# Gates of a token mixer in pairs by seven block products, branch by branch

## The chip, the cores and the metric

The kernel runs on one core of a Trainium2 chip. The core has a matrix engine (TensorE, PE), a vector engine (VectorE, DVE), a scalar engine (ScalarE, ACT), GpSimd (POOL) and a queue engine (SyncE, SP) that here issues DMAs. The metric is device time in microseconds (us). The kernel before takes 2490.34 us, the median of three runs (2489.82 to 2491.25).

## The reference

Two layers over 512 tokens of width 1024, all in 32-bit floats. Each layer is a gated feed-forward block, a token mixer, and a second feed-forward block, each followed by a layer norm. The mixer has three attention branches (a: sparse attention with compressed, selected and windowed keys; b: a sliding window with sinks; c: attention with forget gates), each 512 wide, whose outputs are projected, gated and summed:

```python
q_a, kv_a, g_a, q_b, k_b, v_b, q_c, k_c, v_c, f_c = _split_cols(h @ w_in)
o_a, o_b, o_c = _nsa(...), _swa_sink(...), _fox(...)
g = jax.nn.sigmoid(h @ w_gate + b_gate).reshape(B, S, N_BRANCH, D)
merged = g[:, :, 0] * (o_a @ w_br_a) + g[:, :, 1] * (o_b @ w_br_b) + g[:, :, 2] * (o_c @ w_br_c)
return merged @ w_out
```

`h` is 512 x 1024, `w_gate` 1024 x 3072, each `w_br` 512 x 1024, `w_out` 1024 x 1024. The feed-forward block is `(silu(x @ w1[:, :F]) * (x @ w1[:, F:])) @ w2` with F = 2816.

## The kernel before

**Products of three parts.** A 32-bit operand is held as two parts, `hi` (ACT copies the raw tile to a rounded format) and `lo` (DVE subtracts `hi` from the raw tile). A product of two such operands is three matmuls: hi by hi, hi by the other's lo, lo by hi (`mm3`, L169 to L171). Weights come by DMA on SP into a raw tile 128 x 1024 (`wraw`, three buffers) and are split by `wsplit` (L148 on ACT, L149 on DVE) into a pair of tiles `hi`, `lo` (`unit`: three pairs in the pool `wt`, two more in `wx` where that is open, two more in the feed-forward stage). Activations lie transposed, `xh` and `xl`: 8 planes of 128 features by 512 tokens. A chunk, 128 output columns over all 512 tokens, is 8 planes x 3 = 24 matmuls of 512 columns (`proj`).

**Feed-forward by seven products.** Most column blocks f of the feed-forward stage take their two chunks (gate and up) together. Tokens are cut in two halves and features in two halves; the two chunks are the rows of a 2 x 2 block product, computed with seven block products in place of eight (`seven` and `strassen`). `seven` (L284) loads both chunks' raw tiles `rg` and `ru`, forms sums of halves in two tiles `ws` on DVE (L298 to L301), and splits `rg` (`ug`), the two sums (`u1`, `u2`) and one half of `ru` (`dh`, `dl`). `token_sums` forms the four sums of token halves once per stage and splits them into `th`, `tl`. `strassen` runs the seven products, each 4 planes x 3 matmuls of 256 columns (L361), in three PSUM banks; between them ACT copies a bank to `sn` (L368), and DVE makes the sums `v`, the second chunk `u` and the last addition into the bank (L372 to L380).

**The tail of the mixer.** While the attention runs, gate chunks fill PE between its parts (`chunk`, `pump`): five of each layer's 24, the first block of all three branches (their Tanh goes to `gates0`) and the second block of branches a and b, whose banks are `held`. After the attention comes the tail (L1173 to L1224). The outputs of the three branches are split into `oh`, `ol` (L1208, L1209; 12 tiles each). Then, for each of the 8 blocks d of 128 columns, the three gates (24 matmuls and a Tanh each, L1090; sigmoid is written as a Tanh), and for the branches b, c, a in turn the branch product (`brp`, 4 planes x 3 = 12 matmuls of 512 columns), the gating `(t + 1) * p` on DVE (L1220) and the addition to the block's sum (L1222). The sum is split at once into plane d of `mh` and `ml`, which the product with `w_out` reads (`rows_ln`, L182 to L184): first with planes 0 to 3 over all tokens, then with the other four.

**What sets the order.** PE's and POOL's instructions stand in the order in which the program writes them. Those of DVE, ACT and SP are put in order by a scheduler that sees the whole program; each engine then works strictly through its own list. Buffers are handed on by semaphores: a tile may be written when its slot's last reader is done. SP issues the DMAs of its list one after the other, each when its target is free. [...]

Of the kernel before, what the change touches and what calls it, by code (L numbers as in the profile page):

```python
# [64 lines left out]
def body(tc, a, out, depth=DEPTH):  # L65
# [49 lines left out]
    def wraw(shape=None):  # L115
        return wt.tile(list(shape or [P, KD, P]), F32, name="raw", tag="raw", bufs=3)
# [164 lines left out]
    def ffn_first(w1):  # L281
        return [wcols(w1, c) for c in (0, F, P, F + P)]

    def seven(w1, f):  # L284

        v = w1.rearrange("(k p) f -> p k f", p=P)
        rg = wraw()
        ru = nx.w1.tile([P, KD, P], F32, name="raw", tag="raw") if f % 2 else wraw()  # L290
        nc.sync.dma_start(rg, v[:, :, f * P:(f + 1) * P])
        nc.sync.dma_start(ru, v[:, :, F + f * P:F + (f + 1) * P])
        ug, u1, u2 = wsplit(rg), unit(), unit()
        ud = [nx.w1.tile([P, 4, P], F32R, name=n, tag=n) for n in ("dh", "dl")]
        h1, h2 = slice(0, 4), slice(4, 8)
        x1, x2 = [nx.w1.tile([P, KD, P], F32, name="ws", tag="ws", bufs=2) for _ in range(2)]
        tt = nc.vector.tensor_tensor
        tt(x1[:, h1], ru[:, h1], ru[:, h2], op=OP.add)  # L298
        tt(x1[:, h2], x1[:, h1], rg[:, h1], op=OP.subtract)  # L299
        tt(x2[:, h1], rg[:, h1], ru[:, h1], op=OP.subtract)  # L300
        tt(x2[:, h2], rg[:, h2], x1[:, h2], op=OP.subtract)  # L301
        for (hi, lo), x in ((u1, x1), (u2, x2)):
            nc.scalar.activation(hi, x, AF.Copy)  # L303
            tt(lo, x, hi.bitcast(F32), op=OP.subtract)  # L304
        nc.scalar.activation(ud[0], ru[:, h2], AF.Copy)
        tt(ud[1], ru[:, h2], ud[0].bitcast(F32), op=OP.subtract)
        return ug, u1, u2, ud

    def token_sums(st):

# [17 lines left out]
    def ffn(l, w1, w2, which, xap, xa, wts, pend, done_prev, last, nxt):  # L328
# [20 lines left out]
        H1, H2 = slice(0, 256), slice(256, 512)  # L349

        def strassen(f, ws):
            (ug, u1, u2, ud), (t1, t2, t3, t4) = ws, st.t
            ga, pa, pb = ps(name="pg"), ps(name="pu"), ps(name="pv")
            p_, r_, s_ = [(xh[:, k:k + 4, c], xl[:, k:k + 4, c]) for k, c in ((0, H1), (4, H1), (4, H2))]

            def prod(o, w, k0, x, first=True):
                for k in range(4):
                    hi, lo = w[0][:, k0 + k], w[1][:, k0 + k]
                    vh, vl = x[0][:, k], x[1][:, k]
                    for i, (wx, vx) in enumerate(((hi, vh), (hi, vl), (lo, vh))):  # L360
                        nc.tensor.matmul(o, wx, vx, start=first and k == 0 and i == 0, stop=k == 3 and i == 2,  # L361
                                         skip_group_check=True)

            tt = nc.vector.tensor_tensor
            prod(ga[:, H1], ug, 0, p_)
            prod(ga[:, H2], u1, 0, t1, False)
            sn = st.w1p.tile([P, S], F32, name="sn", tag="sn", bufs=2)
            nc.scalar.activation(sn, ga, AF.Copy)  # L368
            prod(pa[:, H1], u1, 4, t2)
            prod(pa[:, H2], u2, 0, t3, False)  # L370
            v = st.w1p.tile([P, S], F32, name="v", tag="v", bufs=2)
            tt(v[:, H1], pa[:, H1], sn[:, H1], op=OP.add)  # L372
            tt(v[:, H2], pa[:, H2], v[:, H1], op=OP.add)
            prod(pb[:, H1], ud, 0, t4)
            u = hpart(f)
            tt(u[:, H1], pb[:, H1], v[:, H2], op=OP.add)
            tt(u[:, H2], sn[:, H2], v[:, H2], op=OP.add)
            prod(ga[:, H1], ug, 4, r_, False)
            prod(ga[:, H2], u2, 4, s_, False)
            tt(ga[:, H2], ga[:, H2], v[:, H1], op=OP.add)  # L380
            evac(f, ga, u)
# [15 lines left out]
        for f in range(2, KF):  # L397
            if f == KF - 1:
                for k, n in enumerate(("hi", "lo")):
                    h_parts(k, wt.tile([P, KD, P], F32R, name=n, tag=n, bufs=3)  # L400
                            .rearrange("p (a b) c -> p a (b c)", a=2))
            if f not in PLAIN:
                strassen(f, seven(w1, f))
# [70 lines left out]
    def mix(l, wts, pend, done_ffn, xap, xa, nxt):  # L474
# [499 lines left out]
        def chunk(c0, then, w=w_in, load=wcols, bank="mm"):  # L974
            st = K()

            def part(i):
                def go():
                    if i == 0:
                        st.w = load(w, c0)  # L980
                        st.p = ps(bank, "pj")
                    proj(st.p, st.w, ks=range(i, i + 1))
                    if i == 7:
                        then(st.p)
                return go

            fill.extend(part(i) for i in range(8))
# [101 lines left out]
        def gate_ev(t, p, br, d):  # L1089
            nc.scalar.activation(t, p, AF.Tanh, scale=0.5, bias=bg[:, br, d:d + 1])  # L1090

        def gate_chunk(br):
            chunk(br * D, lambda p: gate_ev(gates0[br], p, br, 0), a["w_gate"][l])
# [85 lines left out]
        oh = [[None] * 4 for _ in range(3)]  # L1179
        ol = [[None] * 4 for _ in range(3)]  # L1180
        for br in (1, 2, 0):
            for i in range(4):
                oh[br][i] = ohp.tile([P, S], F32R, name=f"oh{br}{i}")
                ol[br][i] = ohp.tile([P, S], F32R, name=f"ol{br}{i}")
        def wbr(d, brs):
            r = wraw()
            for j, br in enumerate(brs):
                nc.sync.dma_start(r[:, 4 * j:4 * j + 4],
                                  wb[br].rearrange("(k p) f -> p k f", p=P)[:, :, d * P:(d + 1) * P])
            return wsplit(r[:, 0:4 * len(brs)], 4 * len(brs))  # L1190

        def gates(d):
            g_t = []
            for br in range(3):
                if d == 1 and br < 2:
                    p = held[br]
                else:
                    p = ps("sc" if d == 1 else None, "gate")
                    proj(p, wcols(a["w_gate"][l], br * D + d * P))
                t = tp_.tile([P, S], F32, name="t", tag="t", bufs=4)  # L1200
                gate_ev(t, p, br, d)
                g_t.append(t)
            return g_t

        g_1 = gates(1)
        for br in (1, 2, 0):
            for i in range(4):
                nc.scalar.activation(oh[br][i], o_t[br][i], AF.Copy)  # L1208
                nc.vector.tensor_tensor(ol[br][i], o_t[br][i], oh[br][i].bitcast(F32), op=OP.subtract)  # L1209
        for d in range(KD):  # L1210
            g_t = gates0 if d == 0 else g_1 if d == 1 else gates(d)
            for br in (1, 2, 0):
                if br != 2:
                    w = wbr(d, (1, 2) if br else (0,))
                k0 = 4 if br == 2 else 0
                p = ps(name="brp")
                for k in range(4):
                    mm3(p, w, k0 + k, oh[br][k], ol[br][k], k == 0, k == 3)
                t = g_t[br]
                nc.vector.scalar_tensor_tensor(t, t, 1.0, p, op0=OP.add, op1=OP.mult)  # L1220
                if br != 1:
                    nc.vector.tensor_tensor(g_t[1], g_t[1], t, op=OP.add)  # L1222
            nc.scalar.activation(mh[:, d], g_t[1], AF.Copy)
            nc.vector.tensor_tensor(ml[:, d], g_t[1], mh[:, d].bitcast(F32), op=OP.subtract)  # L1224
        ohp.release()
        op.release()
        xap2, xa2 = alloc_xa()
# [146 lines left out]
```

## Time and profile before

| what | value |
|---|---|
| median of 3 runs | 2490.34 us |
| the profiled execution | 2489.96 us, of which the span from first to last instruction is 2488.3 us |
| PE busy | 2470.7 us, 15691 matmuls |
| DVE busy | 1639.8 us |
| ACT busy | 1121.1 us |
| granted TensorE clock | 0.999 |
| tail of the first layer | 683.13 to 851.94 us of the span, 168.81 us |
| feed-forward stage by seven products, first of four | 61.31 to 242.73 us, 181.42 us |

A row of the groups view has the line, engine, operation, output and inputs, shape and count, then busy time in us and the mean of one in ns, then the engine's idle time just before it and what ended it. A row of the waits view has the engine and line that waited, what it waited for, us in total, times, and the longest. A row of the stage table has the stretch in us from the span's start, its length, then each engine's busy time with its instructions, the granted clock, the DMA share and GB/s. A timeline row has the start, the length and the instruction. Matmuls are pipelined and overlap in the record, so it is the distance between starts that counts.

### The profile page before, as it was taken

The page shows a single profiled execution, that of the slowest core. Times are in us where ns is not written, and L with a number is a line of the kernel's source. Part 1 is how long each engine was busy: PE and PEld are TensorE (multiplying, and loading weights), DVE is VectorE, ACT ScalarE, POOL GpSimd, SP SyncE. Part 2 cuts the span into 40 slices and gives each one's busy share as a digit, 9 for nine tenths or more (in the row PEclk, how much of TensorE's full clock was granted, in tenths as well). Part 3 has the DMA queues.
Part 4 walks back from the last instruction along what each step waited for, and adds up shares of the span by engine and source line. Part 5 has one row for each costly group of instructions (what it writes and reads, how often), then busy time and mean ns, then how long its engine had stood idle before and what let it go on. Part 6 is the DMA issues. An engine that isn't in the chain of part 4 may idle for free.

```text
span 2488.3 us, 40610 instructions
## 1 busy us (share of the span) xinstructions
PE 2470.7 (99%) x15691; PEld 2185.0 (88%) x15691; DVE 1639.8 (66%) x3353; ACT 1121.1 (45%) x2148; POOL 228.5 (9%) x454
## 2 busy tenths in 40 slices
PE   9999999999999999999999999999999999999998
PEld 8999887788888889998899998878888888899986
DVE  7897355587654388984579963566776434889734
ACT  4444234577642344443334442345666323444421
POOL 2000110133300000000000000002332000000000
PEclk9999999999999999999999999999999999999999
DMA  6334443633143333334333343445321534333431
GB/s 207 102 102 140 155 128 116 174 86 90 42 141 102 122 122 94 109 111 144 110 102 111 102 160 94 134 120 148 98 77 36 158 95 143 103 102 103 136 119 60
DMA packets 378098, 286.19 MB, mean 115 GB/s; under 512 B 17464, under 2 KB 349384, under 8 KB 377904
## 3 DMA queue, kind: packets, MB, share of 16 engines
q1 hardware_dynamic: 370496, 258.68, 35.6%
q0 software_dynamic: 7408, 24.90, 2.6%
q8 instruction: 124, 2.03, 0.3%
q14 instruction: 70, 0.57, 0.1%
HBM read 256.22 MB, written 17.88 MB: 110 GB/s over the span
## 4 chain that ended last, share of the span: by engine, by line
PE 97%; DVE 2%; DMA 1%; issue 0%; ACT 0%; SPq 0%; DVEq 0%; POOLq 0%; POOL 0%; ACTq 0%
PE pg L361 17%; PE pu L361 8%; PE acc L183 8%; PE acc L184 8%; PE acc L182 8%; PE pj L169 5%; PE pj L170 5%; PE pj L171 5%; PE pv L361 4%; PE gate L169 3%; PE gate L170 3%; PE gate L171 3%; PE brp L169 2%; PE brp L170 2%; PE brp L171 2%; PE sN L888 2%
## 5 line engine op out<-in xcount | busy, mean ns | idle before, releaser
L149 DVE TENSOR_TENSOR lo<-raw,hi 128x1024 fp32r<-128x1024 f32 (+2 forms) x342 | 401.5, 1180 | 478.7 <-ACT hi L148 464.2
L148 ACT ACTIVATE hi<-raw 128x1024 fp32r<-128x1024 f32 (+2 forms) x342 | 347.4, 1023 | 602.1 <-PE acc L183 233.2
L169 PE MATMUL pj<-xh,hi 128*128 128x512 f32 (+1 forms) x720 | 266.9, 371 | 0.4 <-ACT hi L148 0.4
L171 PE MATMUL pj<-xh,lo 128*128 128x512 f32 (+1 forms) x720 | 254.5, 354 | 0.0
L170 PE MATMUL pj<-xl,hi 128*128 128x512 f32 (+1 forms) x720 | 254.4, 353 | 0.1
L182 PE MATMUL acc<-hi,hs 128*128 128x512 f32 x640 | 249.5, 390 | 0.0
L184 PE MATMUL acc<-lo,hs 128*128 128x512 f32 x640 | 249.0, 389 | 0.0
L183 PE MATMUL acc<-hi,hs 128*128 128x512 f32 x640 | 249.0, 389 | 0.0
L361 PE MATMUL pg<-xh,lo 128*128 128x256 f32 x864 | 244.5, 283 | 0.0
L361 PE MATMUL pg<-xl,hi 128*128 128x256 f32 x864 | 244.5, 283 | 0.0
L361 PE MATMUL pg<-xh,hi 128*128 128x256 f32 x864 | 244.5, 283 | 0.0
L303 ACT ACTIVATE hi<-ws 128x1024 fp32r<-128x1024 f32 x144 | 151.9, 1058 | 138.2 <-DVE ws L299 41.5
L304 DVE TENSOR_TENSOR lo<-ws,hi 128x1024 fp32r<-128x1024 f32 x144 | 175.6, 1221 | 29.5 <-ACT hi L303 29.0
L361 PEld LDWEIGHTS pg<-xl,hi 128*128 128x128 f32 x864 | 165.9, 192 | 0.2
L361 PEld LDWEIGHTS pg<-xh,hi 128*128 128x128 f32 x864 | 165.9, 192 | 0.2
L361 PEld LDWEIGHTS pg<-xh,lo 128*128 128x128 f32 x864 | 165.9, 192 | 0.0
L361 PE MATMUL pu<-th,hi 128*128 128x256 f32 x576 | 163.0, 283 | 0.0
L361 PE MATMUL pu<-tl,hi 128*128 128x256 f32 x576 | 163.0, 283 | 0.0
L361 PE MATMUL pu<-th,lo 128*128 128x256 f32 x576 | 163.0, 283 | 0.0
L171 PEld LDWEIGHTS pj<-xh,lo 128*128 128x128 f32 x720 | 136.1, 189 | 19.7
L169 PEld LDWEIGHTS pj<-xh,hi 128*128 128x128 f32 x720 | 136.4, 189 | 16.2 <-issue 3.7
L170 PEld LDWEIGHTS pj<-xl,hi 128*128 128x128 f32 x720 | 136.8, 190 | 11.7 <-DVE xl L1319 0.3
(324 smaller groups left out, 5873.3 us busy)
## 6 DMA issues: line engine op xcount, KB each, us to landing
raw<-in_ffn_w_dram SPq DMA_DIRECT2D x264, 512.0 KB, 3.8
raw<-in_w_in_dram SPq DMA_DIRECT2D x56, 512.0 KB, 3.9
raw<-in_w_gate_dram SPq DMA_DIRECT2D x48, 512.0 KB, 4.0
x_sp<-xa POOLq DMA_DIRECT2D x24, 512.0 KB, 5.8
ks<-hl SPq DMA_DIRECT2D x96, 128.0 KB, 2.4
xa<-x_sp POOLq DMA_DIRECT2D x16, 512.0 KB, 6.3
raw<-in_w_out_dram SPq DMA_DIRECT2D x16, 512.0 KB, 3.6
tab<-bvec SPq DMA_DIRECT2D x16, 256.0 KB, 3.9
```

The source lines that it names most:

```text
L148: nc.scalar.activation(hi[:, c], raw[:, c], AF.Copy)
L149: nc.vector.tensor_tensor(lo[:, c], raw[:, c], hi[:, c].bitcast(F32), op=OP.subtract)
L169: nc.tensor.matmul(o, hi[:, k], vh, start=first, stop=False)
L170: nc.tensor.matmul(o, hi[:, k], vl, start=False, stop=False)
L171: nc.tensor.matmul(o, lo[:, k], vh, start=False, stop=last)
L182: nc.tensor.matmul(o, sh(k)[:, t], hi[:, c], start=k == 0, stop=False)
L183: nc.tensor.matmul(o, sl(k)[:, t], hi[:, c], start=False, stop=False)
L184: nc.tensor.matmul(o, sh(k)[:, t], lo[:, c], start=False, stop=k == nk - 1)
L303: nc.scalar.activation(hi, x, AF.Copy)
L304: tt(lo, x, hi.bitcast(F32), op=OP.subtract)
L361: nc.tensor.matmul(o, wx, vx, start=first and k == 0 and i == 0, stop=k == 3 and i == 2, skip_group_check=True)
L888: nc.tensor.matmul(o[:, 0:nb].rearrange("p k b j -> p (k b j)"), q, kx[:, 2 * b0:2 * (b0 + nb)].rearrange("p a b -> p (a b)"), start=i == ...
```

## The change

The order of the tail becomes branch by branch: all eight blocks of branch b, then of c, then of a. A sum `mf` (8 planes) collects the gated products; `oh` and `ol` hold one branch at a time (`o_split`). Branch b's eight gates stay whole chunks: the first five are the attention's fillers now (three with their Tanh in `gates0`, two `held`), three stand in the tail. Branches c and a, 16 chunks of each layer's 24, go in pairs of neighbouring blocks through the seven products that the feed-forward stage uses; `strassen` is made general for it (`seven_products`, with the pool and the number of buffers of `sn` and `v` as arguments; two in the feed-forward stage as before, one in the tail). The token sums of `xh`, `xl` are formed in four parts (`token_sums_k`) between branch b's products, and their parts `th`, `tl` lie in the tiles `mh`, `ml`, which take the split merged sum only at the end (`merged`). One raw tile now carries two blocks of one branch's weights (`wbr`), where it carried one block of two branches.

```diff
-    def seven(w1, f):
-        v = w1.rearrange("(k p) f -> p k f", p=P)
+    def seven(w, ca, cb, pl, ru):
+        v = w.rearrange("(k p) f -> p k f", p=P)
         rg = wraw()
-        ru = nx.w1.tile([P, KD, P], F32, name="raw", tag="raw") if f % 2 else wraw()
-        nc.sync.dma_start(rg, v[:, :, f * P:(f + 1) * P])
-        nc.sync.dma_start(ru, v[:, :, F + f * P:F + (f + 1) * P])
+        nc.sync.dma_start(rg, v[:, :, ca:ca + P])
+        ru = ru or wraw()
+        nc.sync.dma_start(ru, v[:, :, cb:cb + P])
         ug, u1, u2 = wsplit(rg), unit(), unit()
...
+    def seven_products(ws, t, pl, u, nb):
+        (ug, u1, u2, ud), (t1, t2, t3, t4) = ws, t
+        ga, pa, pb = ps(name="pg"), ps(name="pu"), ps(name="pv")
...
+        prod(ga[:, H1], ug, 0, p_)
+        prod(ga[:, H2], u1, 0, t1, False)
+        sn = pl.tile([P, S], F32, name="sn", tag="sn", bufs=nb)
+        nc.scalar.activation(sn, ga, AF.Copy)
+        prod(pa[:, H1], u1, 4, t2)
+        prod(pa[:, H2], u2, 0, t3, False)
+        v = pl.tile([P, S], F32, name="v", tag="v", bufs=nb)
+        tt(v[:, H1], pa[:, H1], sn[:, H1], op=OP.add)
+        tt(v[:, H2], pa[:, H2], v[:, H1], op=OP.add)
+        prod(pb[:, H1], ud, 0, t4)
+        tt(u[:, H1], pb[:, H1], v[:, H2], op=OP.add)
+        tt(u[:, H2], sn[:, H2], v[:, H2], op=OP.add)
+        prod(ga[:, H1], ug, 4, r_, False)
+        prod(ga[:, H2], u2, 4, s_, False)
+        tt(ga[:, H2], ga[:, H2], v[:, H1], op=OP.add)
+        return ga
...
-        for br in range(3):
-            gate_chunk(br)
-        for br in range(2):
-            chunk(br * D + P, held.append, a["w_gate"][l])
+        for d in range(3):
+            gate_chunk(d)
+        for d in (3, 4):
+            chunk(D + d * P, held.append, a["w_gate"][l])
...
+        oh = [ohp.tile([P, S], F32R, name=f"oh{i}") for i in range(4)]
+        ol = [ohp.tile([P, S], F32R, name=f"ol{i}") for i in range(4)]
+        mf = ohp.tile([P, KD, S], F32, name="mf")
+        th, tl = (x.rearrange("p (i a) (b s) -> p i (a b) s", a=2, b=2) for x in (mh, ml))
+        tsum = [(th[:, i], tl[:, i]) for i in range(4)]
+        def token_sums_k(k):
...
+            tt(x, xk[0], xk[1], op=OP.add)
+            p_, q, r_, s_ = x[:, 0, H1], x[:, 0, H2], x[:, 1, H1], x[:, 1, H2]
+            for i, u, v in ((0, q, p_), (1, s_, t[:, 0]), (2, s_, q), (3, r_, t[:, 1])):
+                tt(t[:, i], u, v, op=OP.subtract)
+            nc.scalar.activation(th[:, :, k], t, AF.Copy)
+            tt(tl[:, :, k], t, th[:, :, k].bitcast(F32), op=OP.subtract)
...
+        def gate_pair(br, d):
+            ws = seven(a["w_gate"][l], br * D + d * P, br * D + (d + 1) * P, ohp, None)
+            u = g_t[br, d + 1] = gtile()
+            p = seven_products(ws, tsum, ohp, u, 1)
+            gate_ev(u, u, br, d + 1)
+            gate(br, d, p)
+        def branch(br, d, w):
+            p = bank("brp")
+            for k in range(4):
+                mm3(p, w, 4 * (d % 2) + k, oh[k], ol[k], k == 0, k == 3)
+            t = g_t.pop((br, d))
+            o = mf[:, d] if br == 1 else t
+            nc.vector.scalar_tensor_tensor(o, t, 1.0, p, op0=OP.add, op1=OP.mult)
+            if br != 1:
+                nc.vector.tensor_tensor(mf[:, d], mf[:, d], t, op=OP.add)
...
+        gate(1, 5)
+        o_split(1)
+        for d in (3, 4):
+            gate(1, d, held[d - 3])
+        branches(1, 0)
+        token_sums_k(0)
+        gate(1, 6)
+        token_sums_k(1)
+        branches(1, 2)
+        gate(1, 7)
+        token_sums_k(2)
+        branches(1, 4)
+        token_sums_k(3)
+        branches(1, 6)
+        for br in (2, 0):
+            for d in range(0, KD, 2):
+                gate_pair(br, d)
+                if d == 0:
+                    o_split(br)
+                if (br, d) == (0, KD - 2):
+                    merged(range(KD - 2))
+                branches(br, d)
+        merged((KD - 2, KD - 1))
```

More of the change, by code (lines that the diff above doesn't have):

```diff
@@ L307, in seven, with prod @@
         return ug, u1, u2, ud
+    def seven_products(ws, t, pl, u, nb):
+        (ug, u1, u2, ud), (t1, t2, t3, t4) = ws, t
+        ga, pa, pb = ps(name="pg"), ps(name="pu"), ps(name="pv")
+        p_, r_, s_ = [(xh[:, k:k + 4, c], xl[:, k:k + 4, c]) for k, c in ((0, H1), (4, H1), (4, H2))]
+        def prod(o, w, k0, x, first=True):
+            for k in range(4):
+                hi, lo = w[0][:, k0 + k], w[1][:, k0 + k]
+                vh, vl = x[0][:, k], x[1][:, k]
+                for i, (wx, vx) in enumerate(((hi, vh), (hi, vl), (lo, vh))):
+                    nc.tensor.matmul(o, wx, vx, start=first and k == 0 and i == 0, stop=k == 3 and i == 2,
+                                     skip_group_check=True)
+        tt = nc.vector.tensor_tensor
+        prod(ga[:, H1], ug, 0, p_)
[14 more added lines that the diff above has]
+        return ga
     def token_sums(st):
@@ L347, in h_parts @@
             hs[k] = t
[L349 to L381, printed above, removed]
         pts = staged(wts, pend)
@@ L402, in ffn @@
             if f not in PLAIN:
-                strassen(f, seven(w1, f))
+                ru = nx.w1.tile([P, KD, P], F32, name="raw", tag="raw") if f % 2 else None
+                ws = seven(w1, f * P, F + f * P, nx.w1, ru)
+                evac(f, seven_products(ws, st.t, nx.w1, hpart(f), 2), hpart(f))
                 continue
@@ L1178, in mix @@
         ohp = pool("ohp", reuse_waits="tile")
-        oh = [[None] * 4 for _ in range(3)]
-        ol = [[None] * 4 for _ in range(3)]
-        for br in (1, 2, 0):
+        oh = [ohp.tile([P, S], F32R, name=f"oh{i}") for i in range(4)]
[3 more added lines that the diff above has]
+        tsum = [(th[:, i], tl[:, i]) for i in range(4)]
@@ new lines, in token_sums_k @@
+        def token_sums_k(k):
+            tt = nc.vector.tensor_tensor
+            x, t = (ohp.tile([P, KD, P], F32, name="ws", tag="ws", bufs=2) for _ in range(2))
+            x = x.rearrange("p (b k) s -> p b (k s)", b=2)
+            t = t.rearrange("p (i k) s -> p i (k s)", i=4)
+            xk = [y.rearrange("p (b k) s -> p k b s", b=2)[:, k].bitcast(F32) for y in (xh, xl)]
+            tt(x, xk[0], xk[1], op=OP.add)
[4 more added lines that the diff above has]
+            tt(tl[:, :, k], t, th[:, :, k].bitcast(F32), op=OP.subtract)
@@ L1182, in mix, with o_split, wbr @@
+        def o_split(br):
             for i in range(4):
-                oh[br][i] = ohp.tile([P, S], F32R, name=f"oh{br}{i}")
-                ol[br][i] = ohp.tile([P, S], F32R, name=f"ol{br}{i}")
-        def wbr(d, brs):
+                nc.scalar.activation(oh[i], o_t[br][i], AF.Copy)
+                nc.vector.tensor_tensor(ol[i], o_t[br][i], oh[i].bitcast(F32), op=OP.subtract)
+        def wbr(br, d):
             r = wraw()
[L1187 to L1224, printed above, removed]
+            v = wb[br].rearrange("(k p) f -> p k f", p=P)
@@ new lines, in wbr, with bank, gtile, gate @@
+            for j in range(2):
+                nc.sync.dma_start(r[:, 4 * j:4 * j + 4], v[:, :, (d + j) * P:(d + j + 1) * P])
+            return wsplit(r)
+        g_t = {(1, d): gates0[d] for d in range(3)}
+        early = deque(["sc", "tp", "sc", "tp", "sc"])
+        def bank(name):
+            return ps(early.popleft() if early else None, name)
+        def gtile():
+            return tp_.tile([P, S], F32, name="t", tag="t", bufs=4)
+        def gate(br, d, p=None):
+            if p is None:
+                p = bank("gate")
+                proj(p, wcols(a["w_gate"][l], br * D + d * P))
+            t = g_t[br, d] = gtile()
+            gate_ev(t, p, br, d)
@@ new lines, in gate_pair @@
+        def gate_pair(br, d):
[6 more added lines that the diff above has]
+            p = bank("brp")
+            for k in range(4):
+                mm3(p, w, 4 * (d % 2) + k, oh[k], ol[k], k == 0, k == 3)
[4 more added lines that the diff above has]
+                nc.vector.tensor_tensor(mf[:, d], mf[:, d], t, op=OP.add)
@@ new lines, in branches, with merged @@
+        def branches(br, d):
+            w = wbr(br, d)
+            branch(br, d, w)
+            branch(br, d + 1, w)
+        def merged(ds):
+            for d in ds:
+                nc.scalar.activation(mh[:, d], mf[:, d], AF.Copy)
+                nc.vector.tensor_tensor(ml[:, d], mf[:, d], mh[:, d].bitcast(F32), op=OP.subtract)
+        gate(1, 5)
[5 more added lines that the diff above has]
+        gate(1, 6)
```

9 lines of the change are left out of this document (5 added, 4 removed).

## The prediction

> **What bounds the kernel now.** I read the page's busy shares first, then the list of what TensorE (PE) waited for over the whole run.
>
> ```profile
> PE 2470.7 (99%) x15691; PEld 2185.0 (88%) x15691; DVE 1639.8 (66%) x3353; ACT 1121.1 (45%) x2148; POOL 228.5 (9%) x454
> ...
> PE xT L1316 <- DMA xa<-in_x_dram: 4.7, 1, 4.7
> PE ptS L778 <- ACT p L519: 0.9, 2, 0.5
> PE cum L607 <- DVE p L517: 0.7, 2, 0.3
> PE pj L169 <- ACT hi L148: 0.4, 1, 0.4
> PE pt L226 <- issue: 0.3, 1, 0.3
> ```
>
> PE waits 7.0 us in 2488.3, and 4.7 of that is the input at the start. So time is set by how many matmuls there are and at what distance they follow each other. A matmul's own duration is no help (they overlap); the distance between starts is. Two stages matter: one feed-forward stage that already works by seven products (first window), and the tail of a mixing layer that the change rewrites (second window).
>
> ```profile
> core 0: us, PE busy (x) PEld busy (x) DVE busy (x) ACT busy (x) POOL busy (x), PEclk, DMA share, GB/s
> 61.31:242.73 181.42, 181.42 (x1513) 181.42 (x1512) 154.40 (x240) 86.78 (x105) 1.11 (x2) 1.00 0.36 106
> 683.13:851.94 168.81, 168.81 (x746) 139.75 (x745) 75.78 (x93) 57.97 (x78) 0.00 (x0) 1.00 0.41 120
> ```
>
> PE is busy for the whole of both. The tail has VectorE (DVE) at 45% and ScalarE (ACT) at 34%; the seven-product stage runs DVE at 85% and ACT at 48% and PE still never stops. The distances come from first and last starts on PE's timeline:
>
> ```profile
> 61.30 0.28 PE L361 MATMUL pg<-xh,hi 128*128 128x256 f32 x1
> ...
> 242.73 0.40 PE L182 MATMUL acc<-hi 128*128 128x512 f32 x1
> ...
> 705.06 0.39 PE L169 MATMUL gate<-xh,hi 128*128 128x512 f32 x1
> ...
> 851.94 0.39 PE L182 MATMUL acc<-hi,mh 128*128 128x512 f32 x1
> ```
>
> Between the first two lie 18 x 84 = 1512 matmuls of 256 columns: 181.43 / 1512 = 0.1200 us each. Between the last two lie 6 x (3 x 24 + 3 x 12) = 648 of 512 columns: 146.88 / 648 = 0.2267 us each. A 256-column matmul thus costs 53% of a 512-column one, not 50%.
>
> **The change on PE.** A gate chunk costs 8 x 3 = 24 matmuls x 0.2267 = 5.44 us, two of them 10.88 us. A pair by seven products costs 7 x 4 x 3 = 84 x 0.1200 = 10.08 us. One pair saves 0.80 us. There are 8 pairs a layer and two layers: 768 matmuls of 512 columns go (174.1 us), 1344 of 256 come (161.3 us): **12.8 us less on PE**. The 8 plain gates a layer (branch b) and the 24 branch products of 12 matmuls stay as they are, only in another order; five gate chunks a layer still fill the attention, so nothing changes there.
>
> **The splits and sums on DVE and ACT.** These run beside PE; they cost nothing as long as they fit and come in time. Durations of the same operations in the two stages (by line and shape; the last four are of the tail):
>
> ```profile
> L304 DVE TENSOR_TENSOR lo<-ws,hi 128x1024 fp32r<-128x1024 f32 x32 | 39.1, 1221 | 8.0 <-ACT hi L303 8.0
> L306 DVE TENSOR_TENSOR dl<-raw,dh 128x512 fp32r<-128x512 f32 x17 | 11.7, 686 | 2.0 <-ACT dh L305 2.0
> L301 DVE TENSOR_TENSOR ws<-raw,ws 128x512 f32<-128x512 f32 x16 | 11.0, 689 | 0.2
> L372 DVE TENSOR_TENSOR v<-pu,sn 128x256 f32<-128x256 f32 x18 | 7.6, 422 | 4.9 <-PE pu L361 4.5 <-ACT hi L303 0.5
> L303 ACT ACTIVATE hi<-ws 128x1024 fp32r<-128x1024 f32 x32 | 33.9, 1060 | 31.3 <-DVE ws L301 9.1 <-PE pg L361 7.3 <-DVE ws L299 5.8
> L368 ACT ACTIVATE sn<-pg 128x512 f32<-128x512 f32 x18 | 10.8, 598 | 18.4 <-PE pg L361 18.4
> L305 ACT ACTIVATE dh<-raw 128x512 fp32r<-128x512 f32 x17 | 10.7, 632 | 23.7 <-PE pv L361 21.9 <-issue 1.8
> ...
> L1090 ACT ACTIVATE t<-gate,bgate 128x512 f32<-128x512 f32 x19 | 12.8, 672 | 0.0
> L1220 DVE SCALAR_TENSOR_TENSOR t<-t,brp 128x512 f32<-128x512 f32 x20 | 13.7, 687 | 16.6 <-PE brp L171 16.1
> L1222 DVE TENSOR_TENSOR t<-t 128x512 f32<-128x512 f32 x13 | 9.0, 690 | 0.2
> L1209 DVE TENSOR_TENSOR ol<-o,oh 128x512 fp32r<-128x512 f32 x12 | 7.4, 685 | 4.0 <-ACT oh L1208 4.0
> ```
>
> A pair with its two branch products takes PE 10.08 + 24 x 0.2267 = 15.52 us. DVE in it: four low parts of 1024 (three of the pair, one of the branch weights) 4.88; four sums of 512, 2.76; `dl` 0.69; five combinations of 256 at 0.42, 2.11; two gatings 1.37; two additions into `mf` 1.38: 13.2 us, 85% of 15.52. ACT: 4 x 1.06 + 0.63 + 0.60 + 2 x 0.67 = 6.8 us, 44%. That is the density at which the feed-forward stage keeps PE full.
>
> **Order and slack.** DVE's order is fixed by the scheduler. Counting from the start of pair n on PE: the second product's weights `u1` are read until 4.3 us (product 3), `ug` until 8.6 (product 6). The next pair takes these slots; whichever of its two sums takes `u1`'s is split by 4.3 + 1.06 + 1.22 = 6.6, then come `v` and `u` (8.3), `dl`, and the split that waits for `ug`'s slot (8.6 + 1.06 + 1.22 = 10.9). PE wants these at 15.5 + 1.4 = 17: about 6 us of slack. With `sn`, `v`, `dh` and `dl` in single buffers each is free again long before its next use (10 us or more). The wait of `prod` 6 for ACT's copy `sn` is the old one. Behind the split that waits for `ug` stand the last sum on `pg`, the gate's Tanh and the branch weights (about 13 us, wanted at 25.6). I take 0 for all of this.
>
> **The opening**, once a layer, is the tightest place. PE does three gates and eight branch products, 3 x 5.44 + 8 x 2.72 = 38.1 us, and before the first pair's second product (39.5 us) DVE must do seven low parts (8.5), four `ol` (2.7), four parts of the token sums (each 1.22 + 4 x 0.42 + 1.22 by the nearest rows: 16.5), six gatings (4.1), four sums and `dl` (3.5): 35.3 us. DVE stood idle 4.0 us just ahead of `ol` before, so it starts early too. Bounds: 0, and, if the 256-wide subtractions of the sums cost the 0.69 of a 512-wide row, 16 x 0.27 = 4.3 more, that is 39.6 and a stall of nearly nothing; allowing half of that 4.3 as a stall, 2 us a layer. I take 0, since the duration nearest in shape is 0.42.
>
> **The end**: the merged sums of blocks 0 to 5 are split (six of 0.69 on DVE) while the last pair's products and branch products run; `mh` planes are free of token sums after products 2 to 5 of that pair, and w_out's first matmul needs block 0 only. Blocks 6 and 7 are wanted 4 x 24 x 0.2267 = 21.8 us or more into w_out. 0.
>
> **DMA.** The tail moves the same bytes, with three raw buffers; SP issues them in order (two rows of the tail's DMA issues, KB each and us to landing, and one wait of the feed-forward stage):
>
> ```profile
> raw<-in_w_gate_dram SPq DMA_DIRECT2D x17, 512.0 KB, 4.4
> xa<-x_sp SPq DMA_DIRECT2D x4, 512.0 KB, 7.1
> ...
> DVE ws L298 <- DMA raw<-in_ffn_w_dram: 1.7, 5, 0.6
> ```
>
> The four reloads of `xa` stand in SP's queue between the two raws of a late pair; at 7.1 us instead of 4.4 they can delay DVE by about 3 us once a layer, inside the 6 us. 0; POOL has nothing in the tail before or after.
>
> **Sum.** Profiled execution 2489.96 us (span 2488.3 and 1.7 around it) - 12.8 = 2477.2. The median of the runs shown, 2490.34, is 0.4 above that execution: **2477.5**.
>
> **Rivals.**
> (a) *Slower: the raw buffer's loop.* `dl` of one pair is the last reader of its second raw; only then may SP load the next one into it, and DVE's next sums stand in its order ahead of gatings, splits and the next `dl`. The loop is landing time D plus seven operations of 0.69, two low parts, one more addition, four of 0.42 and `dl`: D + 10.3. At D = 4.4 it is 14.7, under the 15.52 of PE. At the 7.1 of `xa` it is 17.4: 1.9 us a pair. Slack of 6 us covers three pairs, the other five in two layers cost 19: 2496.5. It turns the sign from D of about 6.5. The row of the feed-forward sums, which waited 1.7 us in all for their raws, speaks against it; that their raws have one buffer more, for it. [...]
> (b) *The opening stalls*: 4 to 6 us in each of the two layers, so a gain of 1 to 5: 2485 to 2489, mostly no measurable change. For it: DVE's 35 of 39 us. Against: its starts lie closer than its durations add up.
> (c) *More gain: seven for eight in full.* If 256 columns cost half of 512, the gain is 174.1 / 8 = 21.8: 2468.6. Against it stand 1512 starts at 0.1200, and weight loads that fill that stage (181.42 of 181.42) but not the tail (139.75 of 168.81). [...]
>
> **How the numbers follow.** Forecast as worked out, stalls up to some 3 us: 0.79. Partial stalls, still faster: 0.07. (b) at its end within 0.2% (5 us, about what a measurement of this kernel can tell from no change): 0.04. (a): 0.09. (c): 0.01. So faster 0.87, same 0.04, slower 0.09. The range goes from 2475.8 (full gain, run spread of 0.7 and a little for the rounding of the distances) to 2484 (twice 2 us of opening and a 2 to 3 us slip).
>
> **What would show it.** Right: in the tail PE busy without a gap, 84 starts at 0.1200 per pair, a tail shorter by 6.4 us in each layer, DVE there at some 80%. Wrong: PE rows that wait for `lo` or `hi` of `ws` in the tail; a DVE wait for raws of w_gate at the sums of `seven` in every pair (a); waits only at the first pair (b); a distance under 0.12 (c). My number fails most easily if single-buffered tiles, or slots taken in another order than I read, tie DVE to PE more closely than counted.

## The result and the profile after

The changed kernel takes 2480.74 us (median of 5 runs, 2478.53 to 2481.72) against 2490.09 (2489.43 to 2491.25): ratio 0.996, 95% interval 0.9945 to 0.9974, so 9.4 us or 0.4% faster. The forecast was 2477.5 with a range of 2475.8 to 2484.0. Ten more runs of the same kernel, beside the experiments, bring it to 2476.24 to 2481.94 with a median of 2478.70 over all 15; the kernel before stayed between 2488.96 and 2491.55 in all its runs. So the gain is real, its size is 8 to 14 us from run to run against the median before, and the question is why it varies.

The busy shares on the page of the changed kernel, and what PE waited for over the whole run:

```profile
PE 2460.1 (99%) x16267; PEld 2204.2 (89%) x16267; DVE 1763.3 (71%) x3569; ACT 1164.3 (47%) x2196; POOL 229.1 (9%) x454
```

```profile
PE xT L1371 <- DMA xa<-in_x_dram: 4.3, 1, 4.3
PE pt L226 <- issue: 1.5, 1, 1.5
PE ptS L780 <- ACT p L521: 0.9, 2, 0.5
PE pj L169 <- ACT hi L148: 0.8, 1, 0.8
PE cum L609 <- DVE p L519: 0.6, 2, 0.3
PE pj L170 <- DVE xl L229: 0.3, 1, 0.3
```

PE is 10.6 us less busy with 576 more matmuls. Nothing of the tail stands among its waits. Three rows are new or larger: the transposes L226 behind the mixer, 1.5 for 0.3, the first projection, 0.8 for 0.4, and L170, 0.3. The stage table of the changed kernel, with the first seven-product feed-forward stage, which now starts at 62.95 us, and the tails of both layers (columns as before):

```profile
core 0: us, PE busy (x) PEld busy (x) DVE busy (x) ACT busy (x) POOL busy (x), PEclk, DMA share, GB/s
62.95:244.37 181.42, 181.42 (x1513) 181.41 (x1512) 154.60 (x240) 86.76 (x105) 1.11 (x2) 1.00 0.36 107
684.78:847.35 162.57, 162.57 (x1034) 148.29 (x1033) 136.29 (x201) 79.30 (x102) 0.00 (x0) 1.00 0.40 118
1913.00:2075.58 162.58, 162.58 (x1035) 148.30 (x1033) 136.37 (x201) 79.31 (x102) 0.00 (x0) 1.00 0.40 118
```

The feed-forward stage is as long as before. Each tail, from the first gate matmul behind the attention to the first of `w_out`, takes 162.57 us for 168.81: 6.24 less, twice, with PE busy throughout, DVE at 84% and ACT at 49%. That makes 12.5 us. The two profiled executions differ by 2489.96 - 2480.83 = 9.13, so 3.35 us came back outside the tails. They lie in two places.

*Behind the first mixer.* On ACT's timeline of the changed kernel (start, length, instruction, and the idle time before it with what ended it):

```profile
1246.39 1.09 ACT L228 ACTIVATE xh<-pt 128x512 fp32r<-128x512 f32 x2 [2.69 <-PE pt L226]
1250.06 1.06 ACT L148 ACTIVATE hi<-raw 128x1024 fp32r<-128x1024 f32 x1 [2.59 <-DMA raw<-in_ffn_w_dram]
1251.03 1.13 ACT L209 ACTIVATE junk<-xa,st 128x1024 bf16<-128x1024 f32 x1
```

ACT stands 2.59 us at the split of the next stage's fourth weight raw, because the transfer has not landed; behind that split in ACT's fixed order stands the layer norm's Square (L209) of the last token block, which starts only at 1251.03 although DVE's work for it ends at 1247.58, and PE's last transposes (L226), which need what is worked out from it, wait 1.5 us (the list says "issue" there; the chain is read off the timelines). In the kernel before the same split waited 1.39 us for its transfer, and PE 0.3.

*At the start.* PE's timeline, changed kernel:

```profile
8.75 0.58 PE L169 MATMUL pj<-xh,hi 128*128 128x256 f32 x1 [0.76 <-ACT hi L148]
9.13 0.41 PE L170 MATMUL pj<-xl,hi 128*128 128x256 f32 x1
9.34 0.45 PE L171 MATMUL pj<-xh,lo 128*128 128x256 f32 x1
9.59 0.41 PE L169 MATMUL pj<-xh,hi 128*128 128x256 f32 x1
9.80 0.41 PE L170 MATMUL pj<-xl,hi 128*128 128x256 f32 x1
```

These first matmuls of 256 columns start 0.21 us apart, not the 0.120 that the prediction counted with. How many of them do so is seen in the number of matmuls in a stretch (stage table of PE alone: the kernel before, then the changed one):

```profile
8.00:12.00 4.00, 3.50 (x24) 1.00 1.08 367
```

```profile
8.00:12.00 4.00, 3.25 (x15) 1.00 1.06 364
```

15 for 24; when the next transposes start (12.31 us before, 13.97 after), the changed kernel is 1.65 us behind. The granted clock column shows 1.00 in both, but the trace's own list of clock stretches begins only at 8.69 us in the kernel before and at 13.83 us in the changed one, and from there on, in both, the distance is 0.120. So what differs is when PE gets its full clock. The DMA engines are as busy in the one stretch as in the other (1.08 and 1.06).

### The profile page after: what moved, and what is told of

It is laid out like the page before. It is cut to its first block, busy times and chain, and to the rows that moved or that the text cites. A ratio compares the mean times of both kernels' runs of the same rounds, so it can differ in the third digit from the quotient of the medians.

```text
span 2479.1 us, 42076 instructions
## 1 busy us (share of the span) xinstructions
PE 2460.1 (99%) x16267; PEld 2204.2 (89%) x16267; DVE 1763.3 (71%) x3569; ACT 1164.3 (47%) x2196; POOL 229.1 (9%) x454
## 5 line engine op out<-in xcount | busy, mean ns | idle before, releaser
L149 DVE TENSOR_TENSOR lo<-raw,hi 128x1024 fp32r<-128x1024 f32 (+1 forms) x318 | 380.5, 1203 | 342.8 <-ACT hi L148 328.1
L148 ACT ACTIVATE hi<-raw 128x1024 fp32r<-128x1024 f32 (+1 forms) x318 | 328.6, 1041 | 455.5 <-PE acc L183 231.5
L322 PE MATMUL pg<-xh,lo 128*128 128x256 f32 x1056 | 298.8, 283 | 0.0
L322 PE MATMUL pg<-xl,hi 128*128 128x256 f32 x1056 | 298.8, 283 | 0.0
L322 PE MATMUL pg<-xh,hi 128*128 128x256 f32 x1056 | 298.7, 283 | 0.0
L305 ACT ACTIVATE hi<-ws 128x1024 fp32r<-128x1024 f32 x176 | 185.8, 1058 | 169.5 <-DVE ws L301 42.1
L170 PE MATMUL pj<-xl,hi 128*128 128x512 f32 (+1 forms) x720 | 255.3, 355 | 0.3 <-DVE xl L229 0.3
L306 DVE TENSOR_TENSOR lo<-ws,hi 128x1024 fp32r<-128x1024 f32 x176 | 214.6, 1221 | 55.1 <-ACT hi L305 54.5
L322 PEld LDWEIGHTS pg<-xh,hi 128*128 128x128 f32 x1056 | 202.7, 192 | 0.8
L322 PEld LDWEIGHTS pg<-xl,hi 128*128 128x128 f32 x1056 | 202.7, 192 | 0.8
L322 PEld LDWEIGHTS pg<-xh,lo 128*128 128x128 f32 x1056 | 202.7, 192 | 0.0
L170 PEld LDWEIGHTS pj<-xl,hi 128*128 128x128 f32 x720 | 137.9, 192 | 11.9 <-DVE xl L229 0.6
```

What stands on the lines that cost most here:

```text
L148: nc.scalar.activation(hi[:, c], raw[:, c], AF.Copy)
L149: nc.vector.tensor_tensor(lo[:, c], raw[:, c], hi[:, c].bitcast(F32), op=OP.subtract)
L170: nc.tensor.matmul(o, hi[:, k], vl, start=False, stop=False)
```

## The experiments

Each kernel is the changed kernel with the edit shown; only the last is the kernel before with an edit. Ratios are to runs of the kernel before on the same chip.

**The change once more.** No edit.

> The changed kernel once more, unaltered. Of the 12.8 us forecast its profile before this run showed 12.5 in the two tails (6.2 each), 1.65 us given back in the first 24 matmuls at 8.7 us of the span (0.213 us apart in place of 0.120) and some 1.3 to 1.5 us at the transposes ahead of the second layer's first feed-forward block. Theory 1 (both givebacks are chance of a run, not of the change): the tails are again 162.5 to 162.6 us, the other two come or go; single times spread over 3 us between 2478 and 2482, difference to before 9 to 12 us. Theory 2 (the change itself causes them, by its other addresses or transfers): both are there again at the same size, difference 9.3 us.

2479.72 us (2476.38 to 2481.94), ratio 0.9958 (0.9945 to 0.997). Its profiled execution was the fastest, 2476.38: there ACT's wait for the raw was 0.71 for 2.59, the row of the transposes L226 is gone from PE's waits, and the tails are again 162.58 each. Its full clock came at 9.40 us. The loss outside the tails is thus not a fixed price of the change.

**The order alone.** The branches one after the other, but all gates as whole chunks and no token sums.

```diff
-        token_sums_k(0)
         gate(1, 6)
-        token_sums_k(1)
...
-                gate_pair(br, d)
+                gate(br, d)
+                gate(br, d + 1)
```

> The new order alone: branch by branch, one set of split outputs, the merged sum split at the end, but all gates of branches a and c as whole chunks of 24 matmuls, and no token sums. Theory 1 (time is the number of matmuls times their distance): the same matmuls as before in another order, tail 168.7 us, time as before within 2 us (2488 to 2492). Theory 2 (the new order itself costs the 3 us that are missing): 3 us slower than before, some 2493.

2493.42 us (2491.51 to 2496.56), ratio 1.0016 (1.0007 to 1.0025): slower by 3.7. The tails don't show it (stage table):

```profile
684.21:853.02 168.81, 168.81 (x746) 139.80 (x745) 76.40 (x89) 57.38 (x74) 0.00 (x0) 1.00 0.38 116
1918.25:2087.06 168.81, 168.81 (x746) 139.80 (x745) 76.39 (x89) 57.36 (x74) 0.00 (x0) 1.00 0.38 116
```

They equal those of before to the hundredth. Its profiled execution is 3.3 us longer than that of the kernel before. Set side by side on PE's timeline, the two show where: 1.5 us at a spell of half the clock from 31.8 to 35.2 us (explained below), and 1.9 and 1.0 us in the layer norms behind `w_out` of the two layers; 1.0 us are won back elsewhere. In the layer norms PE's list of waits names the split of the last transposes:

```profile
PE pj L170 <- DVE xl L229: 1.2, 2, 1.0
```

On DVE's timeline of this kernel the low part of a feed-forward raw, itself late behind its transfer, stands ahead of the layer norm's first step:

```profile
882.51 1.22 DVE L149 TENSOR_TENSOR lo<-raw,hi 128x1024 fp32r<-128x1024 f32 x1 [1.75 <-ACT hi L148]
883.65 0.68 DVE L206 SCALAR_TENSOR_TENSOR xa<-acc,xa 128x512 f32<-128x512 f32 x1
```

So the reordering moves nothing in the tail, and in this kernel it disturbs the stage behind it, with a late weight ahead of the layer norm on DVE. The number came as the second theory had it, but not from one fixed cost: the changed kernel and the one with half of the pairs have no wait of PE between 847 and 1000 us.

**Half of the pairs.** Branch c in pairs, branch a in whole chunks.

```diff
-                gate_pair(br, d)
+                if br == 2:
+                    gate_pair(br, d)
+                else:
+                    gate(br, d)
+                    gate(br, d + 1)
```

> Seven products for branch c's eight gates only, branch a's as whole chunks: 8 pairs in place of 16. Theory 1: half of the tail's gain, 3.2 us a layer, tail 165.6 us; 2490.1 - 6.4 = 2483.7, with the chance of the start 2482 to 2486. Theory 2 (a fixed cost of about 3 us for token sums and order, paid whatever the number of pairs): 2486 to 2487.

2483.29 us (2482.91 to 2486.12), ratio 0.9976 (0.9966 to 0.9986). Its tail:

```profile
684.52:850.21 165.69, 165.69 (x890) 144.02 (x889) 113.45 (x157) 70.54 (x90) 0.00 (x0) 1.00 0.39 118
```

165.69 is the exact middle of 168.81 and 162.57: the gain goes by the number of pairs, 0.78 us each, and nothing is lost at the opening, where these first pairs stand.

**Eight products in halves.** The order of the change, gates of a and c as two half chunks of 256 columns each, so no product is saved; no token sums.

```diff
+        def gate_halves(br, d):
+            p = bank("gate")
+            w = wcols(a["w_gate"][l], br * D + d * P)
+            proj(p, w, H1)
+            proj(p, w, H2)
+            gate(br, d, p)
...
-                gate_pair(br, d)
+                gate_halves(br, d)
+                gate_halves(br, d + 1)
```

> The new order, gates of branches a and c as whole chunks but in two halves of 256 columns: 96 matmuls of 256 columns for a pair, eight products for eight, and no token sums. It measures the price of 256 columns in this stage. Theory 1 (0.1200 us against 0.2267 for 512): 96 x 0.1200 = 11.52 against 10.88 us a pair, 16 pairs: 10.2 us slower than before, 2500. Rival (256 columns cost half of 512): as before, 2490.

2506.49 us (2503.98 to 2508.38), ratio 1.0068 (1.0054 to 1.0081). Its tail:

```profile
685.15:859.25 174.10, 174.10 (x1131) 159.83 (x1129) 76.39 (x89) 57.37 (x74) 0.00 (x0) 1.00 0.37 112
```

5.29 us more than whole chunks in a tail of 16 such gates: 0.33 a gate, where 48 x 0.1200 - 24 x 0.2267 = 0.32 was expected. So a pair saves one product in eight, 12 x 0.120 = 1.44 us, and pays 2 x 0.33 for the narrower matmuls: 0.78. Of the 16.8 us that this kernel is slower than before, 10.6 are the two tails; the rest, which the expected 2500 had not counted, lies at the start and at the layer norms, as in the kernel with the order alone.

**More work on DVE.** Three, then six additions of 128x512 behind each pair, whose result nothing reads.

```diff
                 gate_pair(br, d)
+                jk = ohp.tile([P, S], F32, name="jk")
+                for _ in range(3):
+                    nc.vector.tensor_tensor(jk, mf[:, d], mf[:, d], op=OP.add)
```

> The changed kernel with three more additions of 128 x 512 on DVE in each pair (their result is used by nothing), 2.1 us. DVE then has 13.2 + 2.1 = 15.3 of the pair's 15.5 us. Theory (DVE runs beside PE and has 2.3 us a pair to spare): no change against the changed kernel, 2478 to 2482. Rival (DVE already ties PE): up to 16 x 2.1 = 33 us slower.

> As the last, with six more additions, 4.1 us a pair by their durations: 17.3 of 15.5 us, so DVE is over PE by 1.8 us a pair. Theory: a lead of some 6 us covers three pairs in each layer, the other five pay 1.8 us: 18 us slower than the changed kernel, 2498; by starts that lie closer than durations (0.60 for 0.69) nothing to 5 us.

With three, 2478.5 us (2478.12 to 2481.72), ratio 0.9958 (0.9944 to 0.9971): no change. Its tail has DVE at 91% and the same length:

```profile
686.06:848.64 162.58, 162.58 (x1035) 148.29 (x1033) 147.71 (x225) 78.76 (x102) 0.00 (x0) 1.00 0.40 119
```

With six, 2492.42 us (2489.75 to 2496.53), ratio 1.0011 (1.0002 to 1.002): the whole gain is gone. PE's waits in the tail name one place, once a layer:

```profile
PE pg L322 <- DVE lo L306: 8.4, 2, 4.2
```

It is the second product of the first pair, at 729.39, not a wait in each pair as the theory had it. The additions did not stay behind their pairs: DVE's order is the scheduler's, and `mf` is ready early. DVE's timeline has 16 of the layer's 48 ahead of that product, from 695.78 us on (in the kernel with three, 9 of 24). The stage table of the whole tail, and of the stretch around that wait:

```profile
684.61:854.05 169.44, 165.01 (x1034) 150.31 (x1033) 160.83 (x248) 78.61 (x101) 0.00 (x0) 0.98 0.38 114
727.00:733.80 6.80, 4.41 (x20) 4.42 (x21) 6.80 (x8) 3.55 (x4) 0.00 (x0) 0.50 0.58 157
```

A stall of 4.2 us made the tail 6.87 longer: behind it some 20 matmuls start 0.21 us apart, at a granted clock of 0.50 in that stretch. The opening bore 9 additions more without a wait, and not 16; the pairs behind it bore the other 32, four to five each. That steady pairs bear six is not shown.

**The second raw late.** The second weight raw of each pair in the tail is loaded twice in a row, first with unused columns.

```diff
-        ru = ru or wraw()
+        if not ru:
+            ru = wraw()
+            if pl is not nx.w1:
+                nc.sync.dma_start(ru, v[:, :, ca:ca + P])
```

> The changed kernel with the second raw tile of each pair in the tail loaded twice, first with other columns that nothing reads: its landing comes after about 8 us in place of 4. Rival (a) of the prediction: the loop of landing time + 10.3 us is 18.3 to 19, over PE's 15.5 by 3 us a pair; slack covers two pairs, six pay in each layer: some 35 us slower than the changed kernel, 2515. If the loop is not there (slots taken otherwise, or more slack): as the changed kernel, 2478 to 2482.

2480.39 us (2480.09 to 2485.0), ratio 0.9967 (0.9953 to 0.998). DVE did wait for it in every pair behind the opening (its waits from 722 to 845 us), and the tail grew by 0.74 (stage table):

```profile
DVE ws L303 <- DMA raw<-in_w_gate_dram: 25.1, 7, 4.0
```

```profile
685.58:848.89 163.31, 163.08 (x1035) 148.38 (x1033) 132.83 (x199) 76.59 (x101) 0.00 (x0) 1.00 0.48 139
```

25.1 us of waiting on DVE cost PE less than 1 in the tail: the loop of the raw buffer, by which rival (a) had each pair but the first few pay, is not there.

**One pair more, earlier.** Blocks 6 and 7 of branch b by seven products too, the token sums moved ahead of it.

```diff
         token_sums_k(0)
-        gate(1, 6)
         token_sums_k(1)
         branches(1, 2)
-        gate(1, 7)
         token_sums_k(2)
-        branches(1, 4)
         token_sums_k(3)
+        branches(1, 4)
+        gate_pair(1, 6)
         branches(1, 6)
```

> One pair more in each layer: branch b's blocks 6 and 7 by seven products too, with the four token sums moved ahead. PE: 0.80 us less in each layer, 1.6 in all: 2479 if nothing else moves. Against it: DVE has 35 us of work ahead of the first pair, which now starts 16 us earlier, at 22 us of the tail; if it comes too late PE waits there up to 13 us a layer, and the kernel is up to 25 us slower than the changed one.

2497.19 us (2496.42 to 2498.41), ratio 1.003 (1.0018 to 1.0042). A pair should have made the tail 161.8 us; it is 8.5 longer, since PE waits in each layer at the first pair and the stretch behind runs at a lowered clock (PE's waits, then the stage table):

```profile
PE pg L322 <- ACT hi L305: 11.8, 2, 6.0
```

```profile
685.59:855.92 170.33, 163.97 (x1070) 151.03 (x1069) 142.51 (x212) 81.87 (x105) 0.00 (x0) 0.98 0.38 113
715.00:725.00 10.00, 9.53 (x63) 9.23 (x64) 7.50 (x10) 3.46 (x5) 0.00 (x0) 0.78 0.42 114
```

The two gates taken away were 10.9 us of cover for the token sums and the first pair's splits.

**The late raw behind the mixer.** The fourth weight raw of a feed-forward opening gets a tile of its own, so that it need not wait for one of three raw buffers. Done to the changed kernel and to the kernel before, with the changed kernel once more beside them.

```diff
-        return [wcols(w1, c) for c in (0, F, P, F + P)]
+        ws = [wcols(w1, c) for c in (0, F, P)]
+        r = nx.pool.tile([P, KD, P], F32, name="raw4")
+        nc.sync.dma_start(r, w1.rearrange("(k p) f -> p k f", p=P)[:, :, F + P:F + 2 * P])
+        return ws + [wsplit(r)]
```

> As the changed kernel, but the fourth weight raw of each feed-forward stage's opening has a tile of its own, so that its DMA need not wait until one of the three raw buffers has been split. Theory (part of the gain is lost at the layer norm behind the mixer, because ACT's split of that raw waits for its DMA and stands ahead of the layer norm's Square): in the profile ACT's wait for raw<-in_ffn_w_dram at 1250 us (2.59 in the changed kernel) falls under 0.3, PE's wait at the transposes L226 (1.5) goes back to 0.3, and the time is 1 to 2 us less than the changed kernel's of the same call. Rival (the stall has another cause, or the split waits for something else): the time is within 0.7 us of the changed kernel's and a wait at L226 or L170 of over 1 us is still there.

> The changed kernel once more, beside the two others of this call. Theory: 2479.7 to 2480.7, and its profile has either the wait of 1.5 us at the transposes L226 or not, with a time some 1.5 us apart, as the two profiles so far. Rival (the changed kernel's time is as even as the kernel before's, and its first result of 2480.7 was chance): 2479 within 0.7 in all runs.

> The kernel before with the fourth raw in a tile of its own. Theory (in the kernel before that transfer comes in time, its wait at L226 is 0.3): no change, 2489.2 to 2490.2. Rival (the late transfer costs the kernel before as much): 1 to 2 us less, 2488.

Changed kernel with the extra tile: 2478.18 us (2476.07 to 2479.66), ratio 0.9953 (0.994 to 0.9965). Changed kernel again: 2476.99 (2476.24 to 2481.87), ratio 0.9952 (0.994 to 0.9965). Before with the extra tile: 2490.49 (2488.95 to 2490.72), ratio 0.9999 (0.999 to 1.0008). ACT's timeline of the first, at the place shown above:

```profile
1246.90 1.06 ACT L148 ACTIVATE hi<-raw 128x1024 fp32r<-128x1024 f32 x1 [0.24 <-DMA raw<-in_ffn_w_dram]
1247.87 1.13 ACT L209 ACTIVATE junk<-xa,st 128x1024 bf16<-128x1024 f32 x1
```

The wait falls to 0.24 and PE's row at L226 is gone, as the mechanism wants, but it isn't shown that the extra tile did this. Against the expectation the changed kernel measured beside it came out 1.2 lower in the median, and in its profile, too, the row is gone, with the transfer 0.97 late. In the kernel before, the extra tile took away both waits, 1.39 on ACT and 0.3 on PE, and left the time as it was. What can be said is how late the transfer was (0.71, 0.97 and 2.59 us in three executions of the changed kernel, 1.39 in one of the kernel before), and that PE did not wait in the first two, waited 1.5 us in the third and 0.3 in the last. Six of the changed kernel's 15 runs lie above 2480; none of the five with the extra tile does, which is too few to call it better.

Why the first of these was not at 2476 is seen in the stage table, 28 to 36 us, of it and of the repeated change, and then of the part of the first in which the clock was lowered:

```profile
28.00:36.00 8.00, 8.00 (x58) 7.87 (x57) 6.14 (x7) 1.56 (x3) 0.00 (x0) 0.79 0.70 235
```

```profile
28.00:36.00 8.00, 8.00 (x66) 7.22 (x65) 6.23 (x8) 2.90 (x4) 0.01 (x1) 1.00 0.66 212
```

```profile
31.75:35.10 3.35, 3.35 (x18) 3.35 (x17) 2.39 (x3) 0.00 (x0) 0.00 (x0) 0.50 0.68 198
```

Same instructions, but 58 matmuls for 66 and a granted clock of 0.79 for 1.00, behind 28 small matmuls of 32 columns (28.39 to 31.4 us). It costs 1.5 us. Of the 13 profiled executions 7 have this spell, all of them kernels with the new order of the tail; the three of the changed kernel itself and the two with the old tail have none. Whether the old tail is free of it two executions can't tell.

The kernel before with the extra tile, profiled at 2490.56, got its full clock only at 13.63 us, and its runs fall into 2488.95 to 2489.29 and 2490.21 to 2490.72. The slow start is thus no property of the change (its stage table, PE alone):

```profile
8.00:12.00 4.00, 3.52 (x16) 1.00 1.07 364
```

In the profiles the slow start and the late transfer go together. Ten of them have the new order and three raw buffers. In the five whose full clock came by 10.03 us the transfer is 0.71 to 0.97 late, and PE does not wait at the transposes L226 behind the first mixer. In the five whose full clock came at 12.42 us or later PE waits 1.0 to 1.6 us there, and the transfer is 2.56 to 2.68 late in four of them (0.69 in the kernel with one pair more). What ties the two isn't shown, and the changed kernel with the extra tile was profiled only with an early clock (7.82 us).

## Why the prediction was right, step by step

**PE: 12.8 us. Right, measured 12.5.** Both tails are 6.23 to 6.24 us shorter in every profile of the changed kernel without added work. By the predicted distances the new tail is 360 x 0.2267 + 672 x 0.1200 = 162.25 and the old 744 x 0.2267 = 168.66; measured are 162.57 and 168.81. The 0.17 a layer that was missing lies in the pairs: from the start of one to the start of the next with two branch products it is 15.54 us (723.03 to 847.35 for eight) where 15.52 was counted. The half and the eight-product kernels confirm the gain of a pair and the price of 256 columns apart from each other. In the execution of 2476.99 nothing else was lost on balance: 2489.96 - 2476.99 = 13.0, of which 12.5 are the tails.

**More gain, rival (c): wrong.** The length of the tail leaves no room for a distance under 0.12: (162.57 - 360 x 0.2267) / 672 = 0.1205. With 256 columns at half the price of 512 the gain would have been 21.8 us; the traces show 12.5.

**Splits and sums: 0. Right, but the reason was sized too high.** The 13.2 us of DVE per pair were added up from durations. DVE's timeline of the changed kernel shows that the operations start closer than they are long:

```profile
721.77 0.69 DVE L300 TENSOR_TENSOR ws<-raw 128x512 f32<-128x512 f32 x1 [0.41 <-DMA raw<-in_w_gate_dram]
722.38 0.68 DVE L302 TENSOR_TENSOR ws<-raw 128x512 f32<-128x512 f32 x1
722.98 0.68 DVE L1204 TENSOR_TENSOR ol<-o,oh 128x512 fp32r<-128x512 f32 x1
723.58 0.69 DVE L301 TENSOR_TENSOR ws<-ws,raw 128x512 f32<-128x512 f32 x1
```

0.60 from start to start for 0.69. Twenty-four additions more a layer, 14.4 us at that distance, changed the tail by 0.01. DVE is busy for 84% of the tail, where some 80% was predicted; there was more room beside it than the durations say.

**Order and slack: about 6 us, 0. Right.** Rival (a) had asked 1.9 us a pair for a raw 2.7 us later; with DVE made to wait up to 4.0 us for the second raw in seven pairs the tail lost 0.74 in all. So its loop was counted too long. One reason is shown: its operations were taken at 0.69 and 1.22 apart, and the sums start 0.60 apart. That DVE's gatings and splits need not all stand inside it is only argued.

**The opening: tightest place, 0 (bounds 0 to 2). Right on both.** The stage table of the changed kernel, up to the first pair's second product:

```profile
684.78:724.47 39.69, 39.69 (x183) 33.07 (x182) 36.21 (x53) 21.32 (x29) 0.00 (x0) 1.00 0.38 107
```

DVE was busy 36.2 of 39.7 us (35.3 of 39.5 were counted), PE did not wait, and both kernels whose tail stalled stalled there and nowhere else in the tail. The place was not as tight as the sum of durations made it: it bore 9 additions more, 5.4 us. Rival (b) was the right rival with the wrong price: when the opening did fail, with six additions more, a stall of 4.2 us cost 6.9, and PE's clock was granted at 0.50 from 727.00 to 733.80 us.

**The end, DMA in the tail: 0. Right.** `w_out` starts without a wait, and in the changed kernel DVE waits 2.5 us for weight raws between 722 and 845 us without effect on PE.

**What failed: the sum itself, which ended at the tails.** It took all work outside them as unmoved ("nothing changes there" was said of the attention; the layer norm behind the mixer and the start were not looked at). The first result lay 3.2 us over the forecast. In its profiled execution 1.7 went at the transposes behind the first mixer and 1.65 at the start, where PE got its full clock late; no rival named either. That the result still lay inside the range is in part luck: the room up to 2484 was meant for the opening and a slip in the tail, and neither came. The late clock is shown, and not by the change alone, since the kernel before with the extra tile has it too. The late transfer is shown in the traces as well; what makes it late, the order of SP's queue, the hold on the raw buffers by the tail's last weights, or whatever ties it to the slow start, is open. The forecast was that of an execution without both: the two profiled ones without them took 2476.38 and 2476.99, and two more of the 15 runs are as fast.

## What to carry to other kernels

Where PE never waits, count the matmuls of a change and multiply by the distance of their starts, taken from rows of the same shape in the same trace; here that was right to 0.3 us in 12.8. Sums of durations overstated DVE here (sums of 0.69 us start 0.60 apart): with a busy share of 84% it still took 24 more operations a layer without a loss. But the first use of a new scheme, where its setup and the old work overlap, has to be counted separately; a stall of 4.2 us there cost 6.9. Look at the stage behind the one you change, too: here the splits of its weights stood in the same fixed order, on ACT and on DVE, as the layer norm ahead of it. And where an experiment adds work, look in its trace for where the scheduler put it.

## What the runs showed of the hardware

Behind some stretches in which PE was idle or did little, matmuls of 256 columns started 0.21 us apart in place of 0.120; where the traces list the clock there, it is granted at 0.50. This came after 4.2 and 6.0 us of stall (some 20 matmuls at 0.21 after the first), at the start of the program (1.65 us lost in one execution, hardly any in another; the lists begin only with the full clock there), and, unexpected, after 28 matmuls of 32 columns in which PE counts as busy: 7 of the 13 profiled executions have that spell, between 31.7 and 36.8 us, and the other six, with the same small matmuls, do not. Where it is shown above, in the changed kernel with the extra tile, the spell is some 3.4 us long (8 us at a mean clock of 0.79); around the stall of 4.2 us the clock is at 0.50 for all of the 6.80 us shown. What lowers the clock, and why the spell varies from run to run, is not shown. The matmuls themselves slowed down by 1.78 at that clock and not by 2 (0.213 for 0.120). So the stall had a surcharge: 4.2 us of waiting cost 6.9 us of time.
